# Remainders of two operand sets on VectorE instead of GpSimd, and a product moved within the seven-product unit

## The chip, the cores and the metric

One core of one Trainium2 chip. The time is that of the device for one execution, in microseconds. PE is TensorE, DVE is VectorE, ACT is ScalarE, POOL is GpSimd and SP is SyncE, whose queue issues most of the transfers.

## The reference

A decoder trunk of two layers over 2048 positions of width 1024, in float32:

```python
h = rmsnorm(x, norm_a);  b, c, xin, g = split(h @ w_in_a, 4)
x = x + ((b * causal_conv3(c * xin, conv_a)) * silu(g)) @ w_out_a     # "mixer"
k, v = split(rmsnorm(x, norm_kv) @ w_kv, 2)                           # 8 heads of 64
q, g = split(rmsnorm(x, norm_b) @ w_in_b, 2)
z = q k^T / 8, strictly causal
w = exp(z + reverse_cumsum(log_sigmoid(-z)))                          # stick-breaking, no softmax
x = x + ((w v) * silu(g)) @ w_out_b
return rmsnorm(x, norm_f)
```

## The kernel before

Positions are cut into four chunks of 512, kept transposed (features on partitions). Each float32 product is made of three passes: a number is split into a rounded part "hi" and a remainder "lo" (`split`, line 489: ACT copies hi, then DVE or POOL makes `lo = src - hi`), and hi·hi, hi·lo, lo·hi are added in PSUM. The subtraction that makes lo is the "remainder".

The large products of the mixer (input projections of chunks 0-1 but for two blocks, and all of chunks 2-3), of the output projection `w_out_a` (both pairs of chunks) and of k, q, v and the gate of chunks 0-1 go by pairs: two chunks by two halves of the contraction by two blocks of output columns. `fast_unit` (line 857) multiplies these 2 x 2 blocks with seven products instead of eight. A product is twelve matmuls of 128x128 by 128x512 (four blocks of the contraction, three passes). There are 44 such units: 28 in the mixer (tile names fa_C, fa_B and the like), 8 in the output stage (fa_o) and 8 for the pair's k, q, v and gate (fa_kq, fa_vg).

A unit uses three PSUM banks: `a` (kind lin, 2 buffers), `d` (z, 3) and `e` (wt, 2). In the order before: a11·b11 in a (copied out as c11), s1·t1 in d (copied out as p5), s2·t2 on top in a (copied out as c12), s4·b22 on top in d (added to c12), a12·b21 in e (added to c11), s3·t3 on top in a (added to p5), a22·t4 on top in a, which is itself the last result. The copies are ACT's (in the output stage a DVE add with the residual), the adds are DVE's. `NAMES` (line 772) is the order in which the split weights are loaded.

The right-hand operands (b11, t1, t2, b22, b21, t3, t4; each four blocks of 128x512) are made once for a pair. `fast_rest` does so for the first pair and `fast_operands` (line 736) for the others: the mixer's second pair (`fast_all`), both pairs of the output stage (`out_operands`, keys ('o', 0) and ('o', 2)) and the pair of k, q, v, gate (`pair_operands`, key kq). The last three pass `hold=True`, and for them alone `late` (line 743) is GpSimd. t3 is the block b22 minus b12, t4 is b21 minus t2's block. In the trace the operands made from raw blocks are op_b (b11, b22, b21), the differences op_t (t1 to t4).

The order of the instructions isn't that of the program text. Every operation is recorded under the name of its part (such as "po03", an output unit, or "a24", attention of chunk 2, head 4). `PLAN` gives each part a pair of numbers, from which each operation gets a due key; `places` (line 257) sorts by it, with a key never below those that it depends on. `order` (line 283) then takes, again and again, the operation that could start first by a list of the kernel's own costs, with engines, operands, buffers and the turns that DVE and POOL take; the key decides between equals. So matmuls of different parts stand interleaved on PE, and each engine runs its own list in that order, waiting at run time on semaphores.

After the mixer and the output stage come the pair's k, q, v, gate, the projections of chunks 2 and 3, attention by chunk and head (a00 to a37) mixed with them, the last output projection (o0 to o3, n0 to n2) and `finish` (part e).

Of the kernel before, what the change touches and what calls it, by code (L numbers as in the profile page):

```python
# [25 lines left out]
Q, NPL = 4, 2  # L26
# [8 lines left out]
EPS = 1e-6  # L35

PLAN = {
# [25 lines left out]
}  # L63


# [299 lines left out]
def kernel(  # L365
# [15 lines left out]
    nc = Recorder(tc.nc)  # L381
# [48 lines left out]
    def ld512(nm):  # L430
        return sb.tile([P, CH], F32, name=nm, tag="ld", bufs=NL)
# [57 lines left out]
    def split(hi, lo, src, eng=nc.vector):  # L489
        nc.scalar.copy(hi, src)  # L490
        eng.tensor_sub(lo, src, hi.bitcast(F32))

    def w_tile(nm, kt=Q):

        return sb.tile([P, 2, kt, P], F32R, name=f"whl_{nm}", tag="whl", bufs=NWB)
# [89 lines left out]
    late_acc, late, x_in = {}, {}, {}  # L585
# [90 lines left out]
    def operand(c, nm, k, raw, eng=nc.vector):  # L676

        if k == 0:
            fast_b[c, nm] = []
            other = {"t1": "t4", "t4": "t1"} if c == "kq" else {}  # L680
            home[nm] = list(HOMES[other.get(nm, nm)])
        tag = home[nm].pop(0)
        if tag in ("act", "q2"):
            t = sb.tile([P, 2, CH], F32R, name=f"op_{nm}_{c}_{k}", tag=tag, bufs=BUFS[tag])
            pair = (t[:, 0, :], t[:, 1, :])
        else:
            tags = [tag, home[nm].pop(0)]
            pair = tuple(sb.tile([P, CH], F32R, name=f"op{m}_{nm}_{c}_{k}", tag=tg, bufs=BUFS[tg]) for m, tg in enumerate(tags))
        split(pair[0], pair[1], raw, eng)
        fast_b[c, nm].append(pair)  # L690
# [45 lines left out]
    def fast_operands(key, load, eng, hold=False):  # L736

        def raw(nm, i, kk, tag="og", bufs=KD):
            x = sb.tile([P, CH], F32, name=f"x{nm}_{key}_{kk}", tag=tag, bufs=bufs)
            load(i, kk, x)  # L740
            return x

        late = nc.gpsimd if hold else nc.vector
        a = [raw("b11", 1, k) for k in range(Q)]
        for k in range(Q):
            operand(key, "b11", k, a[k])
        b = []
        for k in range(Q):
            b.append(raw("b12", 0, k, *((("ot", 2) if k < 2 else ("p", 2)) if hold else ())))
            eng.tensor_sub(a[k], b[k], a[k])  # L750
            operand(key, "t1", k, a[k])
        d = []
        for k in range(Q):
            d.append(raw("b22", 0, k + Q))
            eng.tensor_sub(a[k], d[k], a[k])
            operand(key, "t2", k, a[k])
        for k in range(Q):
            operand(key, "b22", k, d[k])
        for k in range(Q):
            if not hold:  # L760
                b[k] = raw("c12", 0, k, "ot", 2)
            eng.tensor_sub(b[k], d[k], b[k])
        d = []
        for k in range(Q):
            d.append(raw("b21", 1, k + Q))
            operand(key, "b21", k, d[k], late)
            operand(key, "t3", k, b[k], late)
        for k in range(Q):
            eng.tensor_sub(d[k], d[k], a[k])
            operand(key, "t4", k, d[k])  # L770

    NAMES = ("a11", "s1", "s2", "s4", "a12", "s3", "a22")

    def combine(a, put, vec=nc.vector):

# [21 lines left out]
    def share(key, d, gain):  # L797
        if gain is not None:
            split_d[key[0]], split_d[key[1]] = [d["a11"], d["a12"]], [d["a21"], d["a22"]]

    def fast_weights(c, nm, key, srcs=None, gain=None):

        w = {}
        if key in split_d:
            for n in NAMES:
                w[n] = w_tile(f"{n}_{nm}")
                nc.sync.dma_start(out=w[n].bitcast(F32), in_=split_d[key][n])
            return w
        kept_w = ("a11", "a12", "a21", "a22") if gain is not None else NAMES
        d = {n: dram.tile([P, 2, Q, P], F32, name=f"sw_{n}_{nm}") for n in kept_w}  # L810
# [16 lines left out]
    def prepare(nm, key, srcs, gain=None):  # L827

        split_d[key] = d = {n: dram.tile([P, 2, Q, P], F32, name=f"sw_{n}_{nm}") for n in NAMES + ("a21",)[:gain is not None]}
        share(key, d, gain)  # L830
# [26 lines left out]
    def fast_unit(c, nm, w, keep=None):  # L857

        def product(bank, wn, bn, start, stop):
            n = 0  # L860
            for k in range(Q):
                for i, m in ((0, 0), (0, 1), (1, 0)):
                    nc.tensor.matmul(bank, w[wn][:, i, k, :], fast_b[c, bn][k][m], start=start and n == 0,
                                     stop=stop and n == 3 * Q - 1, skip_group_check=True)
                    n += 1

        def copy(n, ps):
            t = ld512(f"{n}_{nm}")
            nc.scalar.copy(t, ps)
            return t  # L870

        keep = keep or copy
        a = psum.tile([P, CH], F32, name=f"fa_{nm}", tag="lin", bufs=NLIN)
        d = psum.tile([P, CH], F32, name=f"fd_{nm}", tag="z", bufs=NZ)
        e = psum.tile([P, CH], F32, name=f"fe_{nm}", tag="wt", bufs=NWT)
        product(a, "a11", "b11", True, False)
        c11 = keep("f1", a)
        product(d, "s1", "t1", True, False)
        p5 = keep("f5", d)
        product(a, "s2", "t2", False, False)  # L880
        c12 = keep("f2", a)
        product(d, "s4", "b22", False, True)
        nc.vector.tensor_add(c12, c12, d)
        product(e, "a12", "b21", True, True)
        nc.vector.tensor_add(c11, c11, e)
        product(a, "s3", "t3", False, False)
        nc.vector.tensor_add(p5, p5, a)
        product(a, "a22", "t4", False, True)
        return ((c12, p5), (c11, a))

# [110 lines left out]
    def pair_unit(j, nm):  # L1001
        return fast_unit("kq", nm, fast_weights("kq", nm, *pair(j)))
# [348 lines left out]
```

## Time and profile before

| | before |
|---|---|
| median of 3 runs | 1668.49 us (1667.71 to 1669.75) |
| the profiled execution | 1668.08 us, of which 1666.3 between its first and last instruction |
| granted TensorE clock | 0.994 |
| matmuls on PE | 7828 |
| PE, DVE, ACT, POOL busy | 1621.8, 1331.1, 784.9, 524.7 us |

Times in views of the trace count from the span's start. By them the start lasts to about 150 us, the mixer to about 600 with its last units to 645, the output stage to about 820, the pair's k, q, v and gate to about 980, attention with the projections to about 1600, the tail to the end. A row of a timeline merges instructions of one kind that follow each other (x12). An instruction is busy from its start to its end, even where it stands still within.

### The profile page before, as it was taken

To read this page: it belongs to the slowest core of one execution; us is meant where nothing else is said; L and a number is where in the kernel's file an instruction comes from. 1 tells how busy PE (TensorE), PEld (TensorE's weight loads), DVE (VectorE), ACT (ScalarE), POOL (GpSimd) and SP (SyncE) were. 2 spreads that over 40 slices of the span, in tenths; PEclk is the share of its full clock that TensorE was granted. 3 is DMA by queue.
4 is the path that set the end of the run, shared out by engine and by line. 5 is a ranking of instruction groups with operands and counts; after the bars stand their busy time and mean duration, and the time that the engine had idled before them with its cause. 6 is when DMAs were issued, how large, how long until landed. Compare 5 with 4: busy or idle time off the path is not lost.

```text
span 1666.3 us, 24130 instructions
## 1 busy us (share of the span) xinstructions
PE 1621.8 (97%) x7828; PEld 1335.5 (80%) x7828; DVE 1331.1 (80%) x1944; ACT 784.9 (47%) x1483; POOL 524.7 (31%) x708
## 2 busy tenths in 40 slices
PE   7999999999999999999999999999999999999996
PEld 6877888888888887877778888788788888888875
DVE  6999787895656659394885678798999789999995
ACT  6454443442333324242443445555556466666642
POOL 5421000000000204345731132234535145557442
PEclk9999999999999999999999999999999999999997
DMA  9488887888999999999777899999765678789543
GB/s 278 171 270 283 289 301 240 292 294 300 327 376 331 346 363 339 352 312 329 235 244 251 283 355 327 329 313 276 230 210 190 222 253 254 240 249 347 182 155 117
DMA packets 243822, 460.41 MB, mean 276 GB/s; under 512 B 23024, under 2 KB 96752, under 8 KB 243696
## 3 DMA queue, kind: packets, MB, share of 16 engines
q1 hardware_dynamic: 214336, 400.10, 69.8%
q10 hardware_dynamic: 29200, 58.74, 12.2%
q8 instruction: 62, 1.02, 0.2%
q14 instruction: 64, 0.52, 0.1%
q0 software_dynamic: 160, 0.02, 0.1%
HBM read 287.08 MB, written 171.70 MB: 275 GB/s over the span
## 4 chain that ended last, share of the span: by engine, by line
PE 73%; DVE 12%; DMA 6%; issue 5%; ACT 2%; POOL 1%; SPq 0%; ACTq 0%; POOLq 0%; DVEq 0%
PE fa_C L356 9%; PE fa_B L356 9%; PE av L356 6%; PE z L356 5%; PE wt L356 5%; PE fa_o L356 4%; PE fd_B L356 4%; PE fd_C L356 4%; DVE R L356 4%; PE pob L356 3%; PE fd_o L356 2%; PE fe_C L356 2%; PE pg L356 2%; PE fe_B L356 2%; PE fa_kq L356 2%
## 5 line engine op out<-in xcount | busy, mean ns | idle before, releaser
L356 DVE TENSOR_TENSOR_SCAN R<-R,cy,ones 128x512 f32<-128x512 f32 x192 | 249.2, 1323 | 0.4 <-ACT R L356 0.3
L356 ACT CAST wth<-wt 128x512 fp32r<-128x512 f32 (+2 forms) x320 | 154.7, 526 | 160.4 <-PE wt L356 135.1
L356 DVE TENSOR_TENSOR wtl<-wt,wth 128x512 fp32r<-128x512 f32 (+2 forms) x320 | 180.2, 598 | 18.9 <-ACT wth L356 16.7
L356 PE MATMUL z<-kt,q 128*128 128x512 f32 (+2 forms) x640 | 178.0, 379 | 1.7 <-ACT R L356 1.3
L356 ACT ACTIVATE R<-z 128x512 f32<-128x512 f32 (+2 forms) x320 | 158.4, 547 | 26.5 <-PE z L356 22.7
L356 PE MATMUL wt<-ident,R 128*128 128x128 f32 x1088 | 165.2, 272 | 0.5 <-ACT pbs L356 0.3
L356 PEld LDWEIGHTS wt<-ident,R 128*128 128x128 f32 x1088 | 133.0, 140 | 21.0 <-DVE R L356 0.6
L356 POOL COPY cy<-R 128x1 f32<-128x1 f32 x192 | 99.1, 519 | 140.6 <-DVE R L356 110.9
L356 POOL COPY halo<-p 128x2 f32<-128x2 f32 x32 | 15.3, 479 | 382.0 <-DVE p L356 382.0
L356 PEld LDWEIGHTS z<-kt,q 128*128 128x128 f32 x640 | 110.9, 189 | 19.0 <-ACT R L356 4.2
L356 PE MATMUL av<-wth,vv 128*128 128x512 f32 (+1 forms) x320 | 119.4, 373 | 5.6 <-ACT wth L356 3.3
L356 PE MATMUL av<-wtl,vv 128*128 128x512 f32 (+1 forms) x320 | 122.9, 388 | 1.6 <-DVE wtl L356 1.3
L356 DVE TENSOR_TENSOR_SCAN R<-R,ones 128x256 f32<-128x256 f32 (+3 forms) x128 | 105.6, 854 | 5.2 <-POOL R L356 4.2
L356 PE MATMUL pob<-og,whl_ob 128*128 128x512 f32 x360 | 104.9, 403 | 1.5 <-DVE og L356 1.5
L356 POOL TENSOR_SCALAR_AFFINE_SELECT R<-R 128x128 f32<-128x128 f32 x128 | 72.4, 579 | 88.6 <-ACT R L356 87.0
L356 POOL TENSOR_TENSOR acc_x<-acc_x,sq_x 128x512 f32<-128x512 f32 x52 | 73.5, 1415 | 79.1 <-ACT sq_x L356 74.7
L356 PE MATMUL fa_C<-op_t,whl_s_C 128*128 128x512 f32 x336 | 82.9, 390 | 0.2 <-ACT f_C L356 0.2
L356 PE MATMUL fa_B<-op_t,whl_s_B 128*128 128x512 f32 x336 | 81.9, 390 | 0.0
L356 PEld LDWEIGHTS av<-wth,vv 128*128 128x128 f32 x320 | 60.1, 188 | 23.3 <-ACT wth L356 8.8
L356 PEld LDWEIGHTS av<-wtl,vv 128*128 128x128 f32 x320 | 60.2, 188 | 18.7 <-DVE wtl L356 6.4
L356 PEld LDWEIGHTS pob<-og,whl_ob 128*128 128x128 f32 x360 | 64.3, 189 | 13.2 <-DVE og L356 1.9
L356 PEld LDWEIGHTS fa_C<-op_t,whl_s_C 128*128 128x128 f32 x336 | 62.8, 188 | 13.8 <-ACT f_C L356 0.5
(588 smaller groups left out, 3747.1 us busy)
## 6 DMA issues: line engine op xcount, KB each, us to landing
vv<-v_d ACTq DMA_DIRECT2D x80, 256.0 KB, 4.4
kt<-k_d ACTq DMA_DIRECT2D x80, 256.0 KB, 4.4
sw_s_C<-whl_s_C SPq DMA_DIRECT2D x32, 512.0 KB, 3.7
sw_s_B<-whl_s_B SPq DMA_DIRECT2D x32, 512.0 KB, 3.3
whl_s_o<-sw_s_o SPq DMA_DIRECT2D x32, 512.0 KB, 6.2
q<-q_d ACTq DMA_DIRECT2D x64, 256.0 KB, 6.2
sw_a_C<-whl_a_C SPq DMA_DIRECT2D x24, 512.0 KB, 3.6
sw_a_B<-whl_a_B SPq DMA_DIRECT2D x24, 512.0 KB, 3.1
```

Of the source, the lines that this page charges most:

```text
L356: getattr(o.engine.engine, o.name)(*map(real, o.args), **{k: real(v) for k, v in o.kw.items()})
```

## The change

In the three sets made with `hold=True` the eight remainders of b21 and t3 go to VectorE. In all four sets of `fast_operands` t3's operands come before b21's, and b21 is no longer interleaved with them. In `fast_unit` the product a12·b21, with its add to c11, comes after s3·t3 and its add to p5 instead of before; `NAMES` follows. All pairs of numbers in `PLAN` are new.

```diff
 PLAN = {
-    "m01": (-1372.5, -688.5), "x0": (-728.6, -490.9), "x1": (-781.0, -657.4), "s2": (-159.8, 95.1),
...
-    "e": (1179.3, 2001.7),
+    "m01": (-1000.7, -697.2), "x0": (-579.0, -439.7), "x1": (-1194.1, -947.8), "s2": (-122.8, 197.7),
...
+    "o2": (1476.3, 1495.6), "n2": (704.2, 752.8), "o3": (1793.3, 2658.7), "e": (-610.7, 175.2),
 }
...
-        late = nc.gpsimd if hold else nc.vector
+        late = nc.vector
...
         d = []
         for k in range(Q):
+            operand(key, "t3", k, b[k], late)
+        for k in range(Q):
             d.append(raw("b21", 1, k + Q))
             operand(key, "b21", k, d[k], late)
-            operand(key, "t3", k, b[k], late)
...
-    NAMES = ("a11", "s1", "s2", "s4", "a12", "s3", "a22")
+    NAMES = ("a11", "s1", "s2", "s4", "s3", "a12", "a22")
...
         nc.vector.tensor_add(c12, c12, d)
+        product(a, "s3", "t3", False, False)
+        nc.vector.tensor_add(p5, p5, a)
         product(e, "a12", "b21", True, True)
         nc.vector.tensor_add(c11, c11, e)
-        product(a, "s3", "t3", False, False)
-        nc.vector.tensor_add(p5, p5, a)
         product(a, "a22", "t4", False, True)
```

45 rows, old and new, of the table PLAN are left out of this document.

## The prediction

> **What bounds the kernel now.** I read the page's busy shares first, then busy time by stage, then what TensorE (PE) waited for, then the instructions around each of those waits.
>
> ```profile
> span 1666.3 us, 24130 instructions
> PE 1621.8 (97%) x7828; PEld 1335.5 (80%) x7828; DVE 1331.1 (80%) x1944; ACT 784.9 (47%) x1483; POOL 524.7 (31%) x708
> ```
>
> PE is busy 97% of the span, so 44.5 us is all the idle time that any reordering can win. The next view cuts the span at the program's stages (length; busy us and count of PE, weight loads, DVE, ACT, POOL; clock; DMA).
>
> ```profile
> 0.00:150.00 150.00, 138.05 (x603) 110.61 (x604) 131.63 (x204) 78.62 (x135) 56.40 (x54) 1.00 0.76 245
> 150.00:600.00 450.00, 450.00 (x1990) 371.99 (x1989) 328.08 (x505) 170.12 (x290) 28.66 (x56) 1.00 0.89 312
> 600.00:850.00 250.00, 245.02 (x1084) 197.93 (x1083) 171.91 (x263) 89.50 (x156) 114.44 (x82) 1.00 0.89 309
> 850.00:1000.00 150.00, 148.36 (x685) 120.77 (x684) 101.03 (x152) 66.57 (x122) 34.81 (x53) 1.00 0.84 292
> 1000.00:1600.00 600.00, 591.87 (x3242) 495.76 (x3241) 551.49 (x740) 356.81 (x740) 265.77 (x438) 1.00 0.81 257
> 1600.00:1666.30 66.30, 48.49 (x234) 38.42 (x232) 47.01 (x83) 23.30 (x42) 24.62 (x26) 0.85 0.36 118
> ```
>
> The mixer (150 to 600) has no idle PE at all: the seven-product units done there, most of the 44, can gain nothing. The output and pair stages, where the three changed operand sets are made, lose 4.98 us (600 to 850) and 1.64 us (850 to 1000). The start (11.95), attention (8.13) and the tail (17.81) hold the rest; the change reaches them through the plan alone. PE's longest waits within 600 to 850:
>
> ```profile
> PE fa_kq L356 <- DVE op_t_kq L356: 1.5, 1, 1.5
> PE fa_o L356 <- DVE x L356: 1.2, 2, 0.7
> PE fa_B L356 <- DVE f_B L356: 0.8, 1, 0.8
> PE fa_o L356 <- DVE cv L356: 0.5, 1, 0.5
> PE fd_o L356 <- DVE x L356: 0.4, 1, 0.4
> ```
>
> All are waits for VectorE (DVE), none for POOL. Releaser alone doesn't say which step was late, so here are the places (start, length, engine, instruction, idle before):
>
> ```profile
> 640.56 1.75 POOL L356 TENSOR_TENSOR op_t_('o', 0)_1_5976<-xb_('o', 0)_1_3577,op_t_('o', 0)_1_5976 128x512 fp32r<-128x512 f32 x1
> 641.07 1.79 DVE L356 TENSOR_TENSOR xb_('o', 0)_2_5675<-xb_('o', 0)_2_5909,xb_('o', 0)_2_5675 128x512 f32<-128x512 f32 x1
> 642.79 0.68 DVE L356 TENSOR_TENSOR f_B<-f_B,fa_B 128x512 f32<-128x512 f32 x1
> 642.33 0.39 PE L356 MATMUL fd_o<-op_t_('o', 0)_1_5889,whl_s_o 128*128 128x512 f32 x1
> 643.51 0.74 PE L356 MATMUL fa_B<-op_t,whl_a_B 128*128 128x512 f32 x2 [0.80 <-DVE f_B L356]
> 802.01 0.97 PE L356 MATMUL fa_o<-op_t_('o', 2)_0_6869,whl_a_o 128*128 128x512 f32 x3 [0.56 <-DVE x L356]
> 972.84 1.43 PE L356 MATMUL fa_kq<-op_t_kq,whl_a_kq 128*128 128x512 f32 x5 [0.73 <-DVE f_kq L356]
> ```
>
> The three PE rows with a wait are one step: a22·t4 starts in bank a, and waits for the DVE add that reads s3·t3 out of that bank (p5 += a; at 642.79 f_B<-f_B,fa_B). At 643.51 that add was late because the DVE subtraction before it took 1.79 us beside one of the POOL remainders that move.
>
> **The change part by part.**
>
> *The product moved.* No instruction is added. a12·b21, twelve matmuls into another bank, comes between s3·t3 and a22·t4.
>
> ```profile
> 168.75 2.72 PE fd_B L356 x12
> ```
>
> Twelve matmuls last 2.72 us, 0.227 each, and the DVE add lasts 0.68: even an add that is 1.8 us late fits under them. So all three waits go. What one costs is its idle time and a little more: a matmul's record lasts 0.39 while the next can start after 0.227, so 0.16 us of each wait is drawn as busy. That is 0.80 + 0.56 + 0.73 + 3 x 0.16 = 2.57 us. Bounds: 0 (another wait takes each place) and 2.57; I take 2.57, since the cover is four times the add. What is late next: c11 += e now comes 2.72 us ahead of the end of a22·t4 instead of two products ahead. PE doesn't wait for it unless the next-but-one unit wants bank e, and twelve matmuls again cover the 0.68. Should that cover go, the price is the same 0.7 to 0.95 a unit. In the other 41 units the plan already put some other unit's matmuls into that place, at no idle time; there the edit is worth nothing.
>
> The weights' list follows the products: s3 is loaded before a12.
>
> ```profile
> whl_a_o<-sw_a_o SPq DMA_DIRECT2D x24, 512.0 KB, 6.1
> ```
>
> They are the same seven 512 KB loads a unit on SP's queue, 6.1 us each; one goes past the other, each is needed one product earlier or later, as its product is: 0. In the first pair (in the 0 to 150 stage) the remainders still come b21 before t3 for each k, while s3·t3 is now wanted first: up to four remainders of 0.70 late or early, -2.8 to +2.8; I take 0, because either way both products wait for the same DVE queue.
>
> *The remainders moved.* 24 subtractions (three sets, b21 and t3, four each) go from POOL to DVE.
>
> ```profile
> L356 POOL TENSOR_TENSOR op_t_kq<-xb_kq,op_t_kq 128x512 fp32r<-128x512 f32 x4 | 9.3, 2322 | 5.9 <-ACT op_t_kq L356 5.9
> L356 POOL TENSOR_TENSOR op_b_kq<-xb_kq,op_b_kq 128x512 fp32r<-128x512 f32 x4 | 6.2, 1554 | 5.7 <-ACT op_b_kq L356 5.6
> 637.54 3.06 POOL L356 TENSOR_TENSOR op_t_('o', 0)_0_5964<-xb_('o', 0)_0_3564,op_t_('o', 0)_0_5964 128x512 fp32r<-128x512 f32 x1 [8.54 <-ACT op_t_('o', 0)_0_5964 L356]
> 740.50 1.29 POOL L356 TENSOR_TENSOR op_b_('o', 2)_3_6875<-xb_('o', 2)_7_6806,op_b_('o', 2)_3_6875 128x512 fp32r<-128x512 f32 x1
> L356 DVE TENSOR_TENSOR op_t<-xb,op_t 128x512 fp32r<-128x512 f32 x12 | 8.1, 702 | 0.0
> ```
>
> POOL loses 9.3 + 6.2 us for the pair set and 24.1 for the sixteen others (first and last shown). DVE gains 24 x 0.70 = 16.8 us. But it also gets time back, for the two engines get in each other's way:
>
> ```profile
> 657.59 1.28 POOL L356 TENSOR_TENSOR op_b_('o', 0)_2_6157<-xb_('o', 0)_6_6097,op_b_('o', 0)_2_6157 128x512 fp32r<-128x512 f32 x1
> 657.65 1.77 DVE L356 TENSOR_TENSOR op_t_('o', 0)_0_6125<-xb_('o', 0)_4_5949,op_t_('o', 0)_0_6125 128x512 fp32r<-128x512 f32 x1
> 640.07 1.08 DVE L356 TENSOR_TENSOR cv<-cv,f_B 128x512 f32<-128x512 f32 x1
> 830.41 1.02 DVE L356 TENSOR_TENSOR op_t_kq<-xb_kq,op_t_kq 128x512 fp32r<-128x512 f32 x1 [0.69 <-ACT op_t_kq L356]
> ```
>
> A DVE subtraction that starts just after POOL's lasts 1.77 instead of 0.70: it stands still until POOL is done. Seventeen DVE instructions beside the moved 24 are longer for it (the first at 640.07, the last at 830.41), by 12.8 us together. Bounds of what comes back: 0 and 24 x 1.07 = 25.7. I take 12.8, so DVE's load grows by 4.0 us, over these three stretches:
>
> ```profile
> 636.00:668.00 32.00, 30.73 (x134) 24.79 (x133) 28.35 (x38) 12.12 (x21) 16.12 (x10) 1.00 0.96 337
> 714.00:744.00 30.00, 30.00 (x141) 24.73 (x140) 28.43 (x53) 12.72 (x23) 16.69 (x12) 1.00 0.94 320
> 785.00:835.00 50.00, 47.28 (x201) 36.48 (x200) 41.96 (x52) 25.74 (x46) 34.90 (x23) 1.00 0.69 223
> ```
>
> DVE idles 3.65 + 1.57 + 8.04 = 13.3 us in them, which takes in 4.0. The Trainium skill, page "SBUF — State Buffer", section "Who interferes with whom", says that a VectorE instruction with two SBUF inputs and a GpSimd instruction that reads SBUF exclude each other, and that whichever issues first blocks the other for its whole length. The 1.77 beside the 1.28 agrees, and so does the add out of PSUM at 642.79, which kept 0.68. By that rule in its fullest form, every moved instruction having held DVE up, the 25.7 would come back, DVE would end 8.9 us lighter, and the rival below that blames DVE's queue would lose its ground.
>
> Does PE win by it beyond the 2.57? Only if it waited for a moved remainder or behind one. The longest other wait:
>
> ```profile
> 812.18 1.73 POOL L356 TENSOR_TENSOR acc_x<-acc_x,sq_x 128x512 f32<-128x512 f32 x1
> 812.69 1.77 DVE L356 TENSOR_TENSOR fr_a_kq<-fr_a_kq,fr_a_kq 128x512 f32<-128x512 f32 x1
> 815.11 1.43 PE L356 MATMUL fa_kq<-op_t_kq,whl_s_kq 128*128 128x512 f32 x5 [1.47 <-DVE op_t_kq L356]
> ```
>
> Here POOL's sum of squares held DVE up, which stays, and the operand is t2, which was DVE's before. The waits for x and cv (one of fa_o's two, 0.65; 0.5; 0.4) are for bank-freeing adds in DVE's queue, which now has the remainders in it too. So this part is worth between -3.7 (these four waits gone: 1.47 + 0.65 + 0.5 + 0.4, and 4 x 0.16) and +16.8 (all new DVE work on PE's path); I take 0, nearest the 4.0 that 13.3 us of idle DVE covers. On POOL, the sums of squares and the scaling of x1 that stood behind the 24 start earlier; PE waits for none of them.
>
> *The plan.* Every part has new due times, so the order changes in the start, attention and tail too, without a change in their instructions. Two stretches of 50 us of attention bound this:
>
> ```profile
> 1050.00:1100.00 50.00, 47.44 (x250) 39.16 (x249) 40.61 (x60) 24.47 (x53) 12.66 (x27) 1.00 1.01 329
> 1250.00:1300.00 50.00, 50.00 (x288) 42.85 (x287) 47.55 (x62) 32.83 (x69) 23.75 (x40) 1.00 0.63 203
> ```
>
> The best idles 0, the worst 2.56. All twelve as the best would win 8.1, all as the worst lose 12 x 2.56 - 8.1 = 22.6; I take 0, the mean being 0.68 and nothing in the rows favouring either sign.
>
> *Sum:* 1668.08 (the profiled execution) - 2.57 = 1665.5. The median of the runs, 1668.49, is 0.41 above that execution, so 1665.9.
>
> **The rivals.**
>
> *More than the waits goes.* PE idle understates what PE loses. In the mixer weight loads fill 371.99 of 450 us, 82.7%; at 600 to 850 197.93 of 250. At the mixer's pace those loads would need 197.93 / 0.827 = 239.4 us, so the stage loses 10.6, not 4.98. If freer engines and a plan that no longer has to fill the place after s3·t3 win back most of it, the time is 1658 to 1662. The Trainium skill, page "Trainium Kernel Development and Optimization", section "Performance Expectations", calls the weight loads' busy share a good metric of the distance to the roofline and matmul busy time a bad one. By that rule the 80% of this page would leave a fifth of the span to win; the trace agrees only in part, for the mixer's 82.7% stands with no idle PE.
>
> *Hidden anyway.* The plan fills the three places as it did the 41, or three new waits come: 1667.5 to 1669.5.
>
> *Slower by DVE's queue.* The remainders of a set stand in a burst ahead of an add that frees a bank. A burst of eight is 5.6 us. It decides once more than 2.57 + 3.3 = 5.9 us of the 16.8 falls on PE, that is, more than one whole burst. Two give 11.2 - 2.6: 1677. Against it: 13.3 us of idle DVE, and PE waits there of 1.5 at most.
>
> *Slower by the plan.* Four to five of attention's stretches go from the mean of 0.68 to the worst, 1.9 each: +7.5 to +9.4 against -2.6, so 1673 to 1675.5.
>
> **How the numbers follow.** A measurement here tells about 0.2%, 3.3 us, from no change. Forecast (1663 to 1668): 0.45, of which 0.18 lies under 1665.2. More than the waits: 0.22. Hidden: 0.15. DVE's queue: 0.07. The plan: 0.11. So faster 0.18 + 0.22 = 0.40, same 0.27 + 0.15 = 0.42, slower 0.18. Leaving out the lower part of the second case (0.08), DVE's queue (0.07) and the upper half of the plan's case (0.05) gives 1660 to 1674; the forecast's own range is 1663 to 1668.
>
> **What would show it.** No PE wait of an a22·t4 on the p5 add; PE idle at 600 to 1000 down from 6.62 to about 4.5; remainders op_b and op_t on DVE at 0.69 and none on POOL; POOL down by about 40 us, DVE up by about 4; matmul counts as before. The prediction is wrong if PE's waits for DVE in 600 to 850 grow, if its idle time at 1000 to 1600 leaves 8.1 by more than 3 either way, or if the start's 11.95 or the tail's 17.81 moves by more than 2.

## The result, and the profile after

The changed kernel takes 1655.92 us (median of 3 runs, 1654.49 to 1656.44) against 1668.49: ratio 0.9923 (95% interval 0.9907 to 0.9939), 12.6 us faster. The forecast was 1665.9, the range 1660 to 1674. The profiled execution took 1654.49. First the page of after, then its stages (columns as in the prediction's view by stage: length; busy us and count of PE, weight loads, DVE, ACT, POOL; clock; DMA).

```profile
span 1652.7 us, 24087 instructions
PE 1614.5 (98%) x7828; PEld 1337.6 (81%) x7828; DVE 1334.0 (81%) x1968; ACT 786.0 (48%) x1483; POOL 487.9 (30%) x684
```

```profile
0.00:150.00 150.00, 138.09 (x603) 111.98 (x604) 132.10 (x204) 77.99 (x134) 57.19 (x54) 0.99 0.75 242
150.00:600.00 450.00, 449.69 (x1988) 371.62 (x1987) 322.41 (x506) 170.80 (x290) 34.47 (x56) 1.00 0.89 312
600.00:850.00 250.00, 246.91 (x1096) 201.71 (x1095) 180.16 (x287) 93.60 (x163) 78.32 (x60) 1.00 0.91 322
850.00:1000.00 150.00, 148.18 (x693) 121.73 (x692) 102.20 (x153) 64.46 (x118) 34.44 (x51) 1.00 0.84 290
1000.00:1600.00 600.00, 596.28 (x3285) 502.36 (x3283) 560.98 (x761) 364.16 (x755) 264.61 (x449) 1.00 0.80 255
1600.00:1652.70 52.70, 35.41 (x172) 28.23 (x172) 36.19 (x61) 14.96 (x25) 18.84 (x15) 0.84 0.38 125
```

Read the counts of matmuls, not the busy time. Both kernels have 7828 matmuls. By 600 after has done 2591 against 2593, by 1000 it has done 4380 against 4362, by 1600 7665 against 7604. So nothing is won up to 600, some 4 us between 600 and 1000, and more than that in attention, which neither edit touches. The two profiled spans differ by 13.6 us, and busy time hides more than half of it: PE's idle time falls from 44.5 to 38.2, its busy time from 1621.8 to 1614.5 with the same matmuls.

The ends of matmuls in the profile are modelled; their starts are not. So take every gap from one matmul's start to the next one's, less the median gap behind matmuls of its shape (0.227 us for 512 columns), and sum it in the stage where the gap begins. Worked out from the matmul rows of each trace, in us:

| PE time lost | 0 to 600 | 600 to 1000 | 1000 to 1600 | 1600 to the end | sum |
|---|---|---|---|---|---|
| before | 10.9 | 13.2 | 23.1 | 15.9 | 63.0 |
| after | 11.2 | 9.3 | 17.6 | 11.2 | 49.3 |

The sums differ by 13.7, about as the spans do. 3.9 of it lies in the stages of the edits, 5.5 in attention, 4.7 in the tail. (A wait of 1.4 us in after lies across 1600 and counts in attention.) The matmuls of attention's last product (av) and of the last output projection (pob) show the same from the other side, before and then after (count, shortest, median and longest in ns, first and last start; L356 and L355 are one helper's line, which moves with the length of `PLAN`):

```profile
L356 PE MATMUL av<-wtl,vv x320: 274/389/502, 979.8 to 1634.3; 128*128 128x512 f32 x128, 128*128 128x256 f32 x32
L356 PE MATMUL pob<-og,whl_ob x360: 387/393/497, 1342.3 to 1638.4; 128*128 128x512 f32 x180
```

```profile
L355 PE MATMUL av<-wtl,vv x320: 277/389/501, 988.2 to 1618.0; 128*128 128x512 f32 x128, 128*128 128x256 f32 x32
L355 PE MATMUL pob<-og,whl_ob x360: 387/389/497, 1286.4 to 1625.6; 128*128 128x512 f32 x180
```

After starts this product of attention 8.4 us later and ends it 16.3 us earlier. Its output projection starts 56 us earlier. Both are matters of order, and the order is made from the due times and the program's operations.

### The profile page after: what moved, and what is told of

Read it like the earlier page. It is cut to its first block, busy times and chain, and to the rows that moved or that the text cites. A ratio compares the mean times of both kernels' runs of the same rounds, so it can differ in the third digit from the quotient of the medians.

```text
span 1652.7 us, 24087 instructions
## 1 busy us (share of the span) xinstructions
PE 1614.5 (98%) x7828; PEld 1337.6 (81%) x7828; DVE 1334.0 (81%) x1968; ACT 786.0 (48%) x1483; POOL 487.9 (30%) x684
## 5 line engine op out<-in xcount | busy, mean ns | idle before, releaser
L355 DVE TENSOR_TENSOR_SCAN R<-R,cy,ones 128x512 f32<-128x512 f32 x192 | 247.6, 1316 | 0.9 <-ACT R L355 0.6
L355 ACT CAST wth<-wt 128x512 fp32r<-128x512 f32 (+2 forms) x320 | 154.7, 527 | 159.7 <-PE wt L355 133.2
L355 DVE TENSOR_TENSOR wtl<-wt,wth 128x512 fp32r<-128x512 f32 (+2 forms) x320 | 180.1, 597 | 27.6 <-ACT wth L355 26.0
L355 PE MATMUL z<-kt,q 128*128 128x512 f32 (+2 forms) x640 | 179.7, 378 | 1.0 <-DMA kt<-k_d 0.6
L355 ACT ACTIVATE R<-z 128x512 f32<-128x512 f32 (+2 forms) x320 | 158.7, 548 | 30.8 <-PE z L355 23.7
L355 PE MATMUL wt<-ident,R 128*128 128x128 f32 x1088 | 163.9, 272 | 1.1 <-DVE R L355 1.1
L355 PEld LDWEIGHTS wt<-ident,R 128*128 128x128 f32 x1088 | 132.5, 140 | 20.8 <-DVE R L355 1.8
L355 POOL COPY halo<-p 128x2 f32<-128x2 f32 x32 | 16.1, 503 | 433.5 <-DVE p L355 433.5
L355 POOL COPY cy<-R 128x1 f32<-128x1 f32 x192 | 93.9, 492 | 142.0 <-DVE R L355 135.3
L355 PEld LDWEIGHTS z<-kt,q 128*128 128x128 f32 x640 | 111.7, 189 | 18.7 <-ACT R L355 2.3
L355 PE MATMUL av<-wtl,vv 128*128 128x512 f32 (+1 forms) x320 | 121.6, 384 | 1.8 <-DVE wtl L355 1.8
L355 PE MATMUL av<-wth,vv 128*128 128x512 f32 (+1 forms) x320 | 119.0, 372 | 2.8 <-ACT wth L355 2.3
L355 POOL TENSOR_TENSOR acc_x<-acc_x,sq_x 128x512 f32<-128x512 f32 x52 | 75.2, 1449 | 122.4 <-ACT sq_x L355 113.9
L355 DVE TENSOR_TENSOR_SCAN R<-R,ones 128x512 f32<-128x512 f32 (+3 forms) x128 | 103.9, 844 | 3.0 <-POOL R L355 2.3
L355 PE MATMUL pob<-og,whl_ob 128*128 128x512 f32 x360 | 103.8, 401 | 0.9 <-DVE x L355 0.9
L355 POOL TENSOR_SCALAR_AFFINE_SELECT R<-R 128x128 f32<-128x128 f32 x128 | 72.7, 585 | 107.4 <-ACT R L355 104.2
L355 PE MATMUL fa_C<-op_t,whl_s_C 128*128 128x512 f32 x336 | 83.4, 389 | 0.0
L355 PE MATMUL fa_B<-op_t,whl_s_B 128*128 128x512 f32 x336 | 82.0, 389 | 0.0
L355 PEld LDWEIGHTS av<-wth,vv 128*128 128x128 f32 x320 | 60.1, 188 | 19.3 <-ACT wth L355 6.6
L355 PEld LDWEIGHTS pob<-og,whl_ob 128*128 128x128 f32 x360 | 65.2, 188 | 12.6 <-DVE x L355 1.4
L355 PEld LDWEIGHTS av<-wtl,vv 128*128 128x128 f32 x320 | 60.2, 188 | 17.2 <-DVE wtl L355 5.2
L355 PEld LDWEIGHTS fa_B<-op_t,whl_s_B 128*128 128x128 f32 x336 | 63.0, 188 | 13.2
```

The lines of the kernel that those rows point to most:

```text
L355: getattr(o.engine.engine, o.name)(*map(real, o.args), **{k: real(v) for k, v in o.kw.items()})
```

## The experiments

Three theories: the edits win the time; the new due times are better for any program; or due times fit one program, and what won is that they were sought well for this one ("fit", in the later expectations "search"). Each ratio below is against before, measured on the same chip.

**Each half of the change without the other**, and then after with one edit undone:

```diff
 # plan_only: before, with
-PLAN = {...before...}
+PLAN = {...after...}
 # program_only: after, with
-PLAN = {...after...}
+PLAN = {...before...}
 # after_no_r: after, with
-        late = nc.vector
+        late = nc.gpsimd if hold else nc.vector
 # after_no_o: after, with the products, the operands and NAMES in the order of before
```

plan_only: 

> The program of before (remainders of b21 and t3 on POOL, product a12 x b21 ahead of s3 x t3) with the due times of after. Theory 'edits': the 12.6 us come from the two edits, due times are worth nothing by themselves: 1667 to 1670 us. Theory 'better due times': the new due times are simply better, for any program: 1655 to 1660 us. Theory 'fit': due times are good only for the program that they were sought for, and neither half is worth anything alone: slower than before, 1675 to 1690 us.

program_only: 

> The program of after with the due times of before. 'Edits': 1654 to 1660 us. 'Better due times': 1667 to 1670 us, or 2.6 us less where the three bank waits go. 'Fit': slower than before, 1672 to 1685 us, with PE's new idle time spread over stages that the edits don't touch.

after_no_r: 

> After with the 24 remainders back on POOL; products, operand order and due times as after. If the remainders on DVE carry the gain: 1664 to 1669 us. If they are worth nothing (PE never waited for one): 1654 to 1658 us, with POOL 36 us busier and DVE within 5 us of after.

after_no_o: 

> After with a12 x b21 ahead of s3 x t3 again, b21 ahead of t3 in the operands and the weights' list as before; remainders on DVE, due times of after. If the moved product carries the gain: 1664 to 1672 us, with PE waits of a22 x t4 for the p5 add back. If it is worth nothing: 1654 to 1658 us. 'Fit' expects more than the moved product is worth, since the due times were sought with it: 1668 to 1680 us.

| | median us | ratio, interval | lost 0 to 600 | 600 to 1000 | 1000 to 1600 | tail |
|---|---|---|---|---|---|---|
| plan_only | 1676.8 | 1.0051 (1.0035 to 1.0066) | 16.0 | 21.1 | 24.1 | 12.2 |
| program_only | 1674.9 | 1.0041 (1.0029 to 1.0053) | 11.6 | 17.1 | 24.6 | 16.3 |
| after_no_r | 1656.5 | 0.9927 (0.9902 to 0.9953) | 10.1 | 13.8 | 16.4 | 11.5 |
| after_no_o | 1672.4 | 1.0024 (1.0009 to 1.0038) | 15.9 | 18.9 | 20.8 | 11.3 |

Neither half is worth anything alone: both are slower than before, every run of theirs above every one of before's. "Fit" had both times inside its ranges, though not the place: of program_only's added loss, 3.9 of 6.7 us lies between 600 and 1000, not in stages that the edits leave alone. "Edits" and "better due times", as stated for these two, are out. The tail's gain goes with the due times, whatever the program: 11 to 12 us are lost there with those of after, 16 with those of before. Attention's gain needs both halves. Under the due times of after, the remainders on DVE are worth nothing that can be told (1656.5 against 1655.9). With them back on POOL, POOL is 33.5 us busier and DVE 3.7 less:

```profile
sum 1654.20, PE 1614.30 PEld 1338.49 DVE 1330.35 ACT 785.47 POOL 521.40; mean PE 269.05 PEld 223.08 DVE 221.73 ACT 130.91 POOL 86.90
```

The order of the products is different: undone under the due times of after, it costs 16.5 us, most of it between 600 and 1000 (18.9 lost against 9.3) and a part in the mixer (4.7 more up to 600), where before had no idle PE. plan_only, with the same order of products and the same due times, shows the waits; those of PE between 150 and 600, and two of its matmul rows in the output stage:

```profile
PE fa_B L355 <- DVE f_B L355: 1.8, 1, 1.8
PE fa_C L355 <- DVE p L355: 1.6, 1, 1.6
PE fd_C L355 <- ACT f_C L355: 0.9, 1, 0.9
```

```profile
791.64 1.10 PE L355 MATMUL fa_o<-op_t_('o', 2)_0_6556,whl_s_o 128*128 128x512 f32 x3 [2.01 <-DVE x L355]
811.98 0.73 PE L355 MATMUL fa_o<-op_t_('o', 2)_0_6857,whl_a_o 128*128 128x512 f32 x2 [2.02 <-DVE x L355]
```

The 811.98 row is an a22·t4 behind the p5 add again, with 2.02 idle where before had 0.56 (its row at 802.01). Such a wait costs more than itself. Behind each of these two the granted clock is 0.50 for 3.4 us (792.3 to 795.7 and 812.8 to 816.2), and eight matmuls start 0.427 us apart instead of 0.227, so some 1.6 us more are lost each time. Between 150 and 1600 before and after have no such stretch; plan_only has 27 matmuls in them, after_no_o 24 and program_only 17, about 5, 5 and 3 us by this estimate (0.2 us for each). But this doesn't show that the moved product is worth 16.5 us: it shows that these due times rely on it. The question is what the old order does with due times of its own.

**Both programs with due times sought anew.** For four kernels I changed the due times at random and kept what ended earlier by the kernel's own list of costs (`order`, with nothing measured in it), with the same rule and about the same number of tries; no run shows the number of tries. The program stays word for word; only the numbers in PLAN differ.

```diff
 # before_sought_1, before_sought_2: before, with
-    "m01": (-1372.5, -688.5), ...
+    (sought from before's numbers on; from after's numbers on)
 # after_sought_1, after_sought_2: after, with
-    "m01": (-1000.7, -697.2), ...
+    (sought from after's numbers on; from before's numbers on)
```

before_sought_1: 

> The program of before, word for word, with due times sought anew for it: random changes of them, from those of before on, kept where the kernel's own list of costs ends earlier. Theory 'search': what won 12.6 us was due times sought well for a program, and the edits bring little; then this one lands at 1650 to 1660 us too. Theory 'edits': the moved product makes the difference, and the program of before can't be ordered as well: 1663 to 1669 us, with PE's waits of a22 x t4 back at 3 us or more.

before_sought_2: 

> The same, from the due times of after on (which by themselves made this program slower, 1676.8 us). 'Search': 1650 to 1662 us, within 4 us of the first. 'Edits': 1663 us or more.

after_sought_1: 

> The program of after with due times sought as long in the same way, from those of after on. 'Search': 1648 to 1656 us, within 3 us of the program of before with as much search. 'Edits': 1645 to 1655 us and at least 8 us under the program of before with as much search.

after_sought_2: 

> The same from the due times of before on (which by themselves gave 1674.9 us with this program). 'Search' and 'edits' both expect 1648 to 1658 us; how far it lies from the first shows how much chance is in a search, which the difference between the programs has to be measured against.

| | median us | ratio, interval | lost 0 to 600 | 600 to 1000 | 1000 to 1600 | tail |
|---|---|---|---|---|---|---|
| before_sought_1 | 1654.5 | 0.9926 (0.9904 to 0.9947) | 11.2 | 12.7 | 16.1 | 9.7 |
| before_sought_2 | 1655.6 | 0.9923 (0.9902 to 0.9944) | 9.5 | 8.8 | 19.7 | 9.2 |
| after_sought_1 | 1655.9 | 0.9920 (0.9897 to 0.9943) | 8.8 | 15.4 | 16.7 | 11.1 |
| after_sought_2 | 1659.1 | 0.9946 (0.9928 to 0.9963) | 9.4 | 16.3 | 16.9 | 10.6 |

The program of before, without either edit, becomes as fast as the changed kernel: 0.9926 and 0.9923 against 0.9923. That settles it against "edits", which wanted 1663 or more. Two searches on one program differ by up to 0.26%, more than the programs do; after_sought_2, at 1659.1, lies above what both theories expected of it (1648 to 1658). In before_sought_1 the bank waits are still there, longer than in before (a22·t4 at 644.96 and 839.59):

```profile
644.96 1.42 PE L355 MATMUL fa_B<-op_t,whl_a_B 128*128 128x512 f32 x4 [2.17 <-DVE f_B L355]
839.59 1.65 PE L355 MATMUL fa_kq<-op_t_kq,whl_a_kq 128*128 128x512 f32 x6 [0.99 <-DVE f_kq L355]
```

Its granted clock falls to 0.50 behind the first of them (645.8 to 649.2). It is faster than before all the same, by attention and the tail:

```profile
L355 PE MATMUL av<-wtl,vv x320: 277/389/508, 976.9 to 1620.3; 128*128 128x512 f32 x128, 128*128 128x256 f32 x32
L355 PE MATMUL pob<-og,whl_ob x360: 387/393/497, 1291.8 to 1626.2; 128*128 128x512 f32 x180
```

Here too pob starts some 50 us earlier than in before, and av ends 14 us earlier. An early start of pob isn't enough by itself: in plan_only, which takes longer than before, it starts at 1308.3. Which feature of the order wins attention's time stays open.

**Each edit alone, with due times sought for it**, beside after on one chip, six runs each:

```diff
 # o_sought: before, with the moved product, t3 ahead of b21 and NAMES of after; own due times
 # r_sought: before, with
-        late = nc.gpsimd if hold else nc.vector
+        late = nc.vector
 # and own due times (twice as many tries, the first half on before's program)
```

after_again: 

> After itself, on the same chip as the next two, so that they can be set against it: 1654 to 1657 us.

o_sought: 

> The moved product alone (with t3 ahead of b21 and the weights' list; the 24 remainders stay on POOL), with due times sought for this program. 'Search': 1650 to 1657 us, the same as the program of before with sought due times (1654.5 and 1655.6) within 4 us. If the moved product has a worth of its own that the remainders on DVE had spoilt: under 1650 us.

r_sought: 

> The 24 remainders on DVE alone (products and operands in the order of before), with due times sought for this program. 'Search': 1650 to 1659 us. If the moved product is needed: 1663 us or more.

| | median us | ratio, interval |
|---|---|---|
| after_again | 1653.2 | 0.9906 (0.9891 to 0.9921) |
| o_sought | 1653.5 | 0.9904 (0.9887 to 0.9922) |
| r_sought | 1652.1 | 0.9898 (0.9880 to 0.9915) |

All three are alike; after_again fell just under its expected 1654 to 1657. With due times of their own, the four programs (no edit, either, both) have overlapping intervals, but for after_sought_2, whose interval lies wholly above those of these three; that is the program with both edits. None beats the changed kernel by more than can be told. What the edits might be worth below some 0.3%, the spread of the searches, stays open.

## Why the prediction was wrong

**The step that failed is "The plan".** It put the new order of the start, attention and tail at 0, with 8.1 us (attention's idle time) as the most to be won there. Attention and the tail gave 10.2 of the 13.6. Three things were wrong with the term. The tail: it had no room in the sum, and gave 4.7; attention's 5.5 lies within the 8.1. The rivals: only the slower side of the plan became one, "Slower by the plan"; a faster order of attention and tail had no rival and no chance, though the same rows gave attention up to 8.1. The size: the 8.1 was made from the view by stage, where a stall's end is drawn as busy. By the gaps from start to start those two stages had lost 23.1 + 15.9, against 8.1 + 17.8 by the view, of which 9.3 lies behind the last matmul, where the gaps count nothing. Not all of that can be won: of attention's 23.1, about half (11.8) lies at the 21 waits that the view shows, the rest in uneven spacing without idle time. The text itself corrected for stalls at the bank waits (0.16 us each) and by the weight loads' pace in one rival, and not here; its first bound, 44.5 us as all that an order can win, has the same fault, against 63.0 by the gaps.

"Nothing in the rows favouring either sign" was true of the rows: no trace of before alone shows how good its order is. The runs showed it afterwards: before was far from what its own program allows (0.9923 to 0.9926 with other due times).

**The three bank waits.** The mechanism held, the size was too large: less than half of it came. Of after's waits in a22·t4 these are left:

```profile
346.89 1.43 PE L355 MATMUL fa_B<-op_t,whl_a_B 128*128 128x512 f32 x5 [0.22 <-DVE f_B L355]
642.13 1.20 PE L355 MATMUL fa_B<-op_t,whl_a_B 128*128 128x512 f32 x4 [0.38 <-DVE f_B L355]
803.90 0.96 PE L355 MATMUL fa_o<-op_t_('o', 2)_0_6836,whl_a_o 128*128 128x512 f32 x3 [0.34 <-DVE x L355]
```

0.94 + 3 x 0.16 = 1.42 is left, so 1.15 of 2.57 went. Twelve matmuls of cover were not enough where DVE had other work in front of the add: a remainder of 1.54 us before the add at 641.40, one of 1.79 for the weights before the add at 803.17. Nor was the gain needed: before_sought_1 has more of these waits than before and is as fast as after. Once the order is sought anew, a wait that goes or comes can be made up for elsewhere, so it isn't a term of the sum by itself.

**The remainders.** Forecast at 0, and no difference was measured (after_no_r). DVE was to gain 4.0 us net; it gained 3.7. POOL was to lose 39.6; against after_no_r it lost 33.5, because there the 24 last 36.5 us together, and because POOL's other instructions are 2 us longer in after (487.9 against 485.8). Remainders on DVE aren't free of POOL either. The twelve op_b_kq, of which four are new there, last 1009 ns on average, not the 702 that the forecast charged: eight last 0.68 us, four 1.3 to 1.8:

```profile
L355 DVE TENSOR_TENSOR op_b_kq<-xb_kq,op_b_kq 128x512 fp32r<-128x512 f32 x12 | 11.9, 1009 | 0.4 <-ACT op_b_kq L355 0.3
L355 DVE TENSOR_TENSOR op_t_kq<-xb_kq,op_t_kq 128x512 fp32r<-128x512 f32 x16 | 10.9, 712 | 1.1 <-ACT op_t_kq L355 1.1
```

The mutual blocking that the Trainium skill's page "SBUF — State Buffer" states in "Who interferes with whom" goes on with what stays on POOL: each of the four long ones starts beside a POOL instruction that didn't move (sums of squares at 778.63, 797.40 and 825.26, a gain's product at 820.71). The net charge on DVE agrees with the half that the rows gave, not with the rule in its fullest form (8.9 us lighter).

**The rivals.** "More than the waits goes" named the right sign and nearly the time (1658 to 1662), but the wrong place: the stage at 600 to 850 lost 9.1 before and 5.5 after, 3.6 less and not 6.5 to 10.6. "Slower by DVE's queue" came in one place, and small: in after four t3 remainders and one of b21 run on DVE from 653.24 to 656.25, the add that frees bank a comes behind them, and PE waits 0.96 us at 656.99 (0.56 at this place in after_no_r). "Slower by the plan" is the mechanism that decided, with the other sign; with due times made for another program it comes with its own sign (plan_only 9 us slower, program_only 7). Of the marks named, PE's idle time at 600 to 1000 came out right (4.91 against 4.5), and attention's, 3.72 instead of 8.1, was the one said to show the prediction wrong. The tail's mark stayed silent: by the view its idle time went only from 17.81 to 17.29, and the loss of 4.7 shows in the gaps alone.

## What to carry to other kernels

Where an order is sought by a planner, an edit that comes with a new plan has two causes in it. The test that parts them isn't to undo the edit under the new plan, which charged one edit with 16.5 us that it isn't worth once the old order has due times of its own, but to seek a plan as long for the old program. Look for the room in gaps from one matmul's start to the next, and in every stage that the plan reaches, not only in the stage of the edit.

## What the runs showed of the hardware that I had not expected

PE can be full well below a weight-load share of 100%, and the share depends on the mix of matmuls. The mixer, with no idle time, has 371.99 us of loads in 450, 82.7%; before's attention from 1250 to 1300, also with no idle time, has 42.85 in 50, 85.7%. So 80 and 81% for the whole span are near the ceiling of this mix. And PE's busy time isn't a constant of the program: for the same 7828 matmuls it was 1621.8 in before, 1614.5 in after and 1624.0 in plan_only, since short stalls are counted in it, and in plan_only also the matmuls at half the granted clock. That a wait of 2.0 us is followed by 3.4 us at a granted clock of 0.50 (plan_only, at 791.64 and 811.98) makes a long wait dearer than its idle time.
